# A decoder layer: retention rows scaled per token, and adaLN sums moved from the retention loop to the convolution

## The chip, the cores and the metric

One Trainium2 chip, one core. The metric is the device time of one execution in microseconds; lower is better.

## The reference

One decoder layer in float32 for 2048 tokens of 1024 channels. From a vector c come six rows of 1024 values (shift, scale, gate for each of two sub-layers), as silu(c) times a 1024 x 6144 matrix. The mixer projects the modulated input and splits it into a gated short convolution and a retention of four heads in chunks of 128 tokens; the retention's output is normalised per head, gated, set beside the convolution's, and both go through one output projection. Behind each sub-layer stands a layer norm.

```python
mod = sc @ ada_w[layer] + ada_b[layer]
shift_m, scale_m, gate_m, shift_f, scale_f, gate_f = [...]
h = x * (1.0 + scale_m) + shift_m
...
r = _head_groupnorm(_retention(q, k, v)).reshape(bsz, s, wr)
y_ret = jax.nn.silu(g) * r
return jnp.concatenate([y_conv, y_ret], axis=-1) @ w_out
...
x = _layernorm(DN_ALPHA * x + gate_m * mix, ln1_g[layer], ln1_b[layer])
h = x * (1.0 + scale_f) + shift_f
ff = _swiglu(h, w_gate[layer], w_up[layer], w_down[layer])
x = _layernorm(DN_ALPHA * x + gate_f * ff, ln2_g[layer], ln2_b[layer])
```

## The kernel before

Matrix products are taken in float16 with each operand as a high and a low part, three matmuls for one (`mm3`, lines 127 to 129). Each operand is first scaled by a power of two. `scale_of` (line 106) finds it: per-partition maxima `m` on VectorE (`absmax`, line 87), a matmul that spreads them over all partitions (`all_max`, line 99), a reduction of its result (line 104), three short steps (lines 114 to 117), and 1/s on GpSimd (line 118). `split` (lines 122 and 123) then makes the high part on ScalarE and the low part on VectorE.

The stages in order of time: a start that handles four tiles of 128 tokens while the modulation comes in; the retention loop over tiles t = 4 to 15; the convolution as twelve calls of `conv_pair` (n = 6b + u, two blocks of rows b and six units of weights u), each of 84 matmuls in seven products; the output projection with the first norm; the channel sub-layer.

In the retention loop a round t holds the four projections of tile t (`gemm_ret`), the transposes of q and k of tile t - 1 (`ret_transpose`: `split`, then two transposing DMAs on SP's queue, line 745), its scores (`ret_scores`, lines 127 to 129 at 128 columns, mask at line 759), its state (`ret_kv`, line 768), its output and norm (`ret_y`: products at lines 785 and 788, statistics on VectorE, a power and a product on GpSimd at lines 797 and 799, the gate at line 802, then the maxima), and `ret_part`, which scales and splits the result for the output projection. The scale's inverse goes to `ivr[:, t:t + 1]`, one value for each partition, which `op_half` reads as such. Also in the loop: rotary (lines 726 to 730, VectorE and GpSimd), the planes of the convolution's input (`h_more`, with eight GpSimd instructions at lines 336 to 339), and `bg_step`, twice a round.

`bg_step` does a part of the adaLN product. The matrix comes transposed in pages of 256 rows, 1 MB each; `ada_sum` (line 191) multiplies each half page with silu(c), the row `scrow`, and sums it along the row. Pages 0 to 7 (shift and scale of the mixer) are needed at the start; pages 8 to 23 are the 16 that `bg_step` takes in turn, each load one or two steps ahead of its sum. When they are done, `more_modulation` in round t = 13 adds the bias, makes rows of both gates (`row_of`, line 171) and derives the scale of the channel sub-layer. `ada_sum_pool` (line 452) is the same sum with the product on GpSimd (line 457) and the sum on ScalarE (line 462); the start uses it for two pages.

In the convolution, `cw_split` prepares the weights of unit u + 1 just before `conv_pair` of unit u in the first block: scale, scaling on ScalarE (line 873), four differences on GpSimd (874 to 877), high parts on ScalarE (881), low parts on VectorE (882); they are stored, and the second block loads them (`cw_again`).

SBUF is held as 24 pages of 8 KB a partition, taken from and given back to a list by the program (`page`, `free`); a page taken again makes its new writer wait for the last readers. The order of each engine's instructions is set ahead of time by a planner that goes through the program with costs of its own and takes the earliest traced instruction that it thinks ready (those under `tc.high_priority`, as in `scale_of`, before the others); only the start's order is written out. On the chip every engine and every DMA queue then takes its instructions in that order.

Of the kernel before, what the change touches and what calls it, by code (L numbers as in the profile page):

```python
# [40 lines left out]
def kernel(ctx: ExitStack, tc: tile.TileContext, xT, x, c, adaN, adaT, ada_b, w_ret, w_conv,  # L41
# [15 lines left out]
    def page(dt=F32, at=0):  # L57
        """8 KB a partition; at: which of the free pages, from the one that has been free for longest (0) to the one
        that has become free last (-1)"""
        t = unused.pop(max(-len(unused), min(at, len(unused) - 1)))  # L60
        v = t if dt == F32 else t.bitcast(dt)
        owner[id(v)] = (v, t)
        return v
# [25 lines left out]
    def mcol(n=1):  # L89
        """per-partition maxima, rounded to bfloat16: s leaves a factor of two up to the largest float16"""  # L90
        count[0] += 1
        return small.tile([P, n], BF16, tag=f"m{n}", name=f"m{count[0]}", bufs=4)

    def all_max(g, m, each=False, other=None):
        """g [P, 1]: the largest of m [P, n] bfloat16, on every partition; each: of every column, g [P, n]"""
# [10 lines left out]
    def scale_of(m, s, iv, each=False, room=0, other=None):  # L106
        """m: per-partition maxima; s = 2^(14 - room) / 2^floor(log2(max)), iv = 1 / s, both on every partition;
        each: one for every column of m"""
# [11 lines left out]

    def split(src, hi, lo, s):
# [3 lines left out]
    def mm3(ps, l_hi, l_lo, r_hi, r_lo, start, stop, again=False):  # L125
        """again: adds to a sum that has been read"""
# [38 lines left out]
    def row_of(cols, dst, scale):  # L165
        """dst [P, D]: the columns' values as a row on every partition, times scale"""
# [34 lines left out]
    def adan_sum(i):  # L201
        """two columns of mod as a row on the tensor engine, then turned"""
# [71 lines left out]
    def bound(mx, sh, k0=0, k1=KT):  # L274
        """a bound of |x (1 + scale) + shift| on each partition; mx: maxima of |x|, sh: of |shift|"""
# [42 lines left out]
    def h_scale():  # L318
        """one scale for the input's tiles from 8 on and for the convolution's part"""
        scale_of(bound(xall, shm), hs[:, 0:1], hs[:, 1:2], room=2)  # L320

    def h_split(src, s):
        """src: channels' tiles by a pair's 256 rows; parts by tile, by half of the channels, high and low"""
# [7 lines left out]
    def h_sums(src):  # L331
        """of the quarters A11, A12 (even tile), A21, A22: S2 for A11, S4 for A12, S3 for A21, S1 for A22, with
        S1 = A21 + A22, S2 = S1 - A11, S3 = A11 - A21, S4 = A12 - S2"""
# [7 lines left out]
    # planes for the convolution's products, in their order: A11, A12, S4, A22, S1, S2, S3  # L341
# [43 lines left out]
    def h_again(p):  # L385
        """the planes of one of the first pairs"""
# [8 lines left out]
    # The first four tiles in two groups of rows, each with its own scales, as the modulation comes in; the order in  # L395
    # which the engines take this part is that of the program.
# [8 lines left out]
    def ret_half_max(u, i):  # L405
        """unit 1 on ScalarE: sums of |w|, which are at least the maxima"""
# [15 lines left out]
    def ret_half_scale(u, i):  # L422
        """the second half gets the scale of both, the first half its own for the time being"""
# [20 lines left out]
    def ret_rescale(u):  # L444
        """the first half on the scale of both"""
# [6 lines left out]
    def ada_sum_pool(i):  # L452
        """as ada_sum, on GpSimd and ScalarE; the sums when later[i] is stepped"""
# [31 lines left out]
    def start_scale(g, p, other):  # L485
        """other: what is done while the maxima are on their way"""
# [13 lines left out]
    def start_gemm(u, g, t):  # L500
        """a third of the products at a time, those with the weights' low part last"""
# [37 lines left out]
    def in_order():  # L539
        """the engines' instructions of this block in the order in which they stand here"""  # L540
# [26 lines left out]
    with in_order():  # L567
        # some matmuls only keep the array busy until the modulation has come in, for its full clock
# [138 lines left out]
    def qk_scales(p, ivh):  # L707
        """scales that bring q and k of a pair of tiles into float16's range, whatever the products are; the scale of
        q stays on the scores, the sums and the squares that the normalisation's epsilon goes to"""
# [23 lines left out]
    def ret_transpose(t):  # L733
        """q and k, split, with the channels on the partitions, and q once more in one piece"""
# [45 lines left out]
    def ret_y(t):  # L780
# [24 lines left out]
        m = mcol()  # L805
        r = tt[:, 1536:2048]
        absmax(m, r)
        RM[t] = m

    def ret_part(t):  # L810
        r = T1[t][:, 1536:2048]
        s = col(1, "s")
        scale_of(RM.pop(t), s, ivr[:, t:t + 1])
# [29 lines left out]
    # Two tiles of columns at a time, B.1 and B.2; planes in the order of the products: B11, B21, B22, B21 - T2, T1, T2,  # L843
    # T3 with T1 = B12 - B11, T2 = B22 - T1, T3 = B22 - B12.
# [46 lines left out]
    nl, nw = [8], [8]  # L891

    def bg_step():
        if nl[0] < 24 and nl[0] <= nw[0] + 1:
            ada_load(nl[0], -1)
            nl[0] += 1
        if nw[0] < nl[0] - 1 or nl[0] == 24 and nw[0] < 24:
            ada_sum(nw[0])
            nw[0] += 1

# [1 line left out]
    gmp = []  # L902

# [954 lines left out]
```

## Time and profile before

| | us |
|---|---|
| median of 3 runs | 2157.56 |
| lowest and highest | 2155.71, 2157.85 |
| span of the profiled execution | 2156.5 |
| TensorE busy in it | 2032.1 |
| VectorE, GpSimd, ScalarE busy | 1473.8, 1015.5, 672.3 |

The span is from the first to the last instruction of one profiled execution; the profile gives no other time for that execution, so the runs' median stands for what lies around it. In the rows below PE is TensorE, PEld its weight loads, DVE VectorE, ACT ScalarE, POOL GpSimd and SP the queue that issues most DMAs; L99 is line 99 of the kernel; `<-` names what ended an idle time. A row of windows has the stretch and its length, then busy us (and instructions) of PE, PEld, DVE, ACT and POOL, then the granted clock as a share of the full one, the DMA share and GB/s.

### The profile page before, as it was taken

The page shows a single profiled execution, that of the slowest core. Times are in us where ns is not written, and L with a number is a line of the kernel's source. Part 1 is how long each engine was busy: PE and PEld are TensorE (multiplying, and loading weights), DVE is VectorE, ACT ScalarE, POOL GpSimd, SP SyncE. Part 2 cuts the span into 40 slices and gives each one's busy share as a digit, 9 for nine tenths or more (in the row PEclk, how much of TensorE's full clock was granted, in tenths as well). Part 3 has the DMA queues.
Part 4 walks back from the last instruction along what each step waited for, and adds up shares of the span by engine and source line. Part 5 has one row for each costly group of instructions (what it writes and reads, how often), then busy time and mean ns, then how long its engine had stood idle before and what let it go on. Part 6 is the DMA issues. An engine that isn't in the chain of part 4 may idle for free.

```text
span 2156.5 us, 24675 instructions
## 1 busy us (share of the span) xinstructions
PE 2032.1 (94%) x9647; PEld 952.7 (44%) x9647; DVE 1473.8 (68%) x1787; ACT 672.3 (31%) x724; POOL 1015.5 (47%) x771
## 2 busy tenths in 40 slices
PE   8899887899999998999999999999999989996998
PEld 3355444554444443344444444444444434442443
DVE  7888788777684668778655667767663483686554
ACT  5522334444321223332232333334342211212220
POOL 4554566556422477642332444545441183378234
PEclk9999999999999999999999999999999999998999
DMA  9054666496744297655211343343442745464311
GB/s 374 27 141 144 200 187 207 135 285 222 241 178 142 81 263 191 172 174 200 100 62 56 101 153 117 135 144 122 156 140 71 268 160 197 159 238 149 145 70 78
DMA packets 185429, 344.29 MB, mean 160 GB/s; under 512 B 117856, under 2 KB 117856, under 8 KB 162656
## 3 DMA queue, kind: packets, MB, share of 16 engines
q1 hardware_dynamic: 176832, 326.72, 46.2%
q10 hardware_dynamic: 8480, 15.99, 2.1%
q8 instruction: 75, 1.23, 0.2%
q14 instruction: 42, 0.34, 0.0%
HBM read 222.87 MB, written 92.54 MB: 146 GB/s over the span
## 4 chain that ended last, share of the span: by engine, by line
PE 33%; DVE 10%; POOL 8%; DMA 5%; issue 4%; ACT 2%; SPq 0%; POOLq 0%; DVEq 0%; ACTq 0%
PE ax L127 6%; PE ax L129 6%; PE ax L128 6%; PE mm L129 5%; PE mm L127 5%; PE mm L128 5%; DMA wscr<-pg 2%; ACT pg L1504 1%; DVE pg L1453 1%; DVE pg L1505 1%; DVE pg L1457 1%; DMA pg<-yscr 1%; DVE pg L1497 1%; POOL pg L1258 1%; POOL x L118 1%
## 5 line engine op out<-in xcount | busy, mean ns | idle before, releaser
L127 PE MATMUL mm<-pg,pg 128*128 128x512 f16 x1732 | 660.8, 382 | 30.7 <-ACT pg L122 19.9
L128 PE MATMUL mm<-pg,pg 128*128 128x512 f16 x1732 | 661.0, 382 | 0.0
L129 PE MATMUL mm<-pg,pg 128*128 128x512 f16 x1732 | 658.2, 381 | 1.9 <-DVE pg L882 1.0
L128 PEld LDWEIGHTS <-pg 128*128 128x128 f16 x2888 | 284.8, 99 | 362.5 <-issue 38.0
L127 PEld LDWEIGHTS <-pg 128*128 128x128 f16 x2888 | 284.7, 99 | 350.7 <-ACT pg L122 20.5
L129 PEld LDWEIGHTS <-pg 128*128 128x128 f16 x2888 | 284.6, 99 | 337.1 <-issue 5.6
L127 PE MATMUL ax<-pg,pg 128*128 128x512 f16 x1092 | 414.2, 379 | 15.0 <-DVE t2k L1440 15.0
L128 PE MATMUL ax<-pg,pg 128*128 128x512 f16 x1092 | 414.6, 380 | 0.0
L129 PE MATMUL ax<-pg,pg 128*128 128x512 f16 x1092 | 412.4, 380 | 0.0
L1449 POOL TENSOR_TENSOR pg<-pg,t2k 128x512 f32<-128x512 f32 x44 | 59.8, 1359 | 331.1 <-DVE t2k L1448 331.1
L123 DVE SCALAR_TENSOR_TENSOR pg<-pg,p2s,pg 128x2048 f16<-128x2048 f32 (+1 forms) x42 | 117.7, 2809 | 112.3 <-ACT pg L122 108.6
L122 ACT ACTIVATE pg<-pg,p2s 128x2048 f16<-128x2048 f32 (+1 forms) x42 | 77.4, 1856 | 241.4 <-PE mm L128 88.2
L87 DVE TENSOR_REDUCE m<-pg 128x2 bf16<-128x2048 f32 (+2 forms) x54 | 97.0, 1805 | 11.9 <-DMA pg<-in_w_gu_dram 8.8
L517 PE MATMUL mm<-pg,pg 128*128 128x512 f16 x384 | 89.3, 387 | 5.6 <-DVE pg L525 2.5
L1505 DVE TENSOR_TENSOR pg<-pg,pg 128x2048 f16<-128x2048 f32 (+1 forms) x22 | 49.6, 2255 | 52.8 <-ACT pg L1504 52.8
L1456 ACT ACTIVATE pg<-t2k,ivg 128x512 f32<-128x512 f32 x44 | 31.5, 716 | 151.4 <-DVE t2k L1455 151.4
L1448 DVE TENSOR_TENSOR t2k<-ax,t2k 128x512 f32<-128x512 f32 x22 | 15.2, 690 | 82.0 <-PE ax L129 82.0
L1387 ACT ACTIVATE pg<-pg 128x2048 f16<-128x2048 f32 x22 | 42.0, 1909 | 86.5 <-PE ax L128 86.5
L191 DVE SCALAR_TENSOR_TENSOR pg<-pg,pg 128x1024 f32<-128x1024 f32 x40 | 57.1, 1462 | 14.6 <-DMA pg<-in_adaT_dram 14.2
L1504 ACT ACTIVATE pg<-pg 128x2048 f16<-128x2048 f32 (+1 forms) x22 | 37.3, 1697 | 95.0 <-DMA wscr<-pg 60.5
L1558 POOL TENSOR_TENSOR pg<-pg,pg 128x2048 f32<-128x2048 f32 (+1 forms) x6 | 26.9, 4490 | 82.0 <-DMA pg<-uscr 36.4
L118 POOL TENSOR_SCALAR x<-x 128x2 f32<-128x2 f32 x22 | 37.2, 1690 | 59.7 <-DVE x L116 59.5
(273 smaller groups left out, 2893.3 us busy)
## 6 DMA issues: line engine op xcount, KB each, us to landing
pg<-wscr SPq DMA_DIRECT2D x28, 1024.0 KB, 4.9
pg<-in_w_gu_dram SPq DMA_DIRECT2D x22, 1024.0 KB, 4.8
uscr<-pg SPq DMA_DIRECT2D x44, 512.0 KB, 2.7
pg<-in_w_dn_dram SPq DMA_DIRECT2D x22, 1024.0 KB, 5.6
pg<-in_adaT_dram SPq DMA_DIRECT2D x21, 1024.0 KB, 6.5
wscr<-pg SPq DMA_DIRECT2D x77, 256.0 KB, 2.9
pg<-uscr SPq DMA_DIRECT2D x16, 1024.0 KB, 5.8
pg<-in_xT_dram SPq DMA_DIRECT2D x14, 1024.0 KB, 5.3
```

The source lines that it names most:

```text
L87: return nc.vector.tensor_reduce(dst, src, axis=AX.X, op=OP.max, apply_absolute_value=True).ins
L118: nc.gpsimd.tensor_scalar(iv, e, float(2.0 ** (room - 14)), None, op0=OP.mult)
L122: nc.scalar.activation(hi, src, AF.Copy, scale=s)
L123: nc.vector.scalar_tensor_tensor(lo, src, s, hi, op0=OP.mult, op1=OP.subtract)
L127: nc.tensor.matmul(ps, l_hi, r_hi, start=start, stop=False, skip_group_check=again)
L128: nc.tensor.matmul(ps, l_hi, r_lo, start=False, stop=False, skip_group_check=again)
L129: nc.tensor.matmul(ps, l_lo, r_hi, start=False, stop=stop, skip_group_check=again)
L191: nc.vector.scalar_tensor_tensor(v, v, 1.0, scrow, op0=OP.mult, op1=OP.mult, accum_out=mod[:, j:j + 1])
L517: nc.tensor.matmul(ps, hv[:, a, k, o], w[:, k], start=n == 0 and k == k0, stop=n == 2 and k == k1 - 1)
L1449: nc.gpsimd.tensor_add(e5, e5, p1)
L1504: nc.scalar.activation(o[:, :n, 0], src, AF.Copy)
L1505: nc.vector.tensor_sub(o[:, :n, 1], src, o[:, :n, 0])
```

## The change

Two things. First, `ret_part` no longer calls `scale_of`. The maxima of `ret_y` are kept in float32 and a new function makes a scale for each partition, that is for each token, out of its own maximum, on VectorE with 1/s on GpSimd. Second, `bg_step` is gone. The 16 pages are loaded and summed in the convolution: two loads at n = 0; in each of n = 1 to 8 one page is summed on VectorE and one on GpSimd and ScalarE, and each is followed by the load of the next but one. `more_modulation` is cut in two: the mixer's gate row at n = 3, the rest at n = 9. `crow`, the page with silu(c), is given back at n = 8 instead of in round 13. Comments were taken out too, so line numbers differ by a few.

```diff
+    def row_scale(m, s, iv):
+        nc.vector.tensor_scalar(m, m, float(2.0 ** -100), None, op0=OP.max)
+        mi = m.bitcast(I32)
+        nc.vector.tensor_scalar(mi, mi, EXPMASK, None, op0=OP.bitwise_and)
+        nc.vector.tensor_scalar(s.bitcast(I32), mi, -1.0, SBASE, op0=OP.mult, op1=OP.add)
+        nc.gpsimd.tensor_scalar(iv, m, float(2.0 ** -14), None, op0=OP.mult)
...
-        m = mcol()
-        r = tt[:, 1536:2048]
-        absmax(m, r)
+        m = col(1, "g")
+        absmax(m, tt[:, 1536:2048])
         RM[t] = m
...
-        scale_of(RM.pop(t), s, ivr[:, t:t + 1])
+        row_scale(RM.pop(t), s, ivr[:, t:t + 1])
...
-    nl, nw = [8], [8]
-
-    def bg_step():
-        if nl[0] < 24 and nl[0] <= nw[0] + 1:
-            ada_load(nl[0], -1)
-            nl[0] += 1
-        if nw[0] < nl[0] - 1 or nl[0] == 24 and nw[0] < 24:
-            ada_sum(nw[0])
-            nw[0] += 1
...
+    def ada_sum_both(i):
+        ada_sum_pool(i)
+        for _ in later.pop(i):
+            pass
+
+    def mix_modulation():
+        gmp.append(page())
+        ada_bias(16, 24)
+        row_of(mod[:, 2 * KT:3 * KT], gmp[0][:, :D], 1.0 / ALPHA)
+
     def more_modulation():
-        gmp.append(page())
-        ada_bias(16, 48)
+        ada_bias(24, 48)
         nc.vector.tensor_scalar(msc[:, 1], mod[:, 4 * KT:5 * KT], 1.0, None, op0=OP.add)
-        gm = gmp[0][:, :D]
-        row_of(mod[:, 2 * KT:3 * KT], gm, 1.0 / ALPHA)
         row_of(mod[:, 5 * KT:6 * KT], gfrow, 1.0 / ALPHA)
...
         ret_transpose(t - 1)
-        bg_step()
         gemm_ret(t, 1)
...
         ret_y(t - 1)
-        bg_step()
-        if t == NT - 3:
-            free(crow)
-            more_modulation()
...
+            if n == 0:
+                ada_load(8, -1)
+                ada_load(9, -1)
+            if 1 <= n <= 8:
+                ada_sum(6 + 2 * n)
+                if n < 8:
+                    ada_load(8 + 2 * n, -1)
+                ada_sum_both(7 + 2 * n)
+                if n < 8:
+                    ada_load(9 + 2 * n, -1)
+                else:
+                    free(crow)
+            if n == 3:
+                mix_modulation()
+            if n == 9:
+                more_modulation()
             if n == 1:
                 ret_scores(NT - 1)
```

## Rows read from the trace of the kernel before

**Rows 1.** The page: span, busy time of TensorE, its granted clock in 40 slices.

```profile
span 2156.5 us, 24675 instructions
...
PE 2032.1 (94%) x9647; PEld 952.7 (44%) x9647; DVE 1473.8 (68%) x1787; ACT 672.3 (31%) x724; POOL 1015.5 (47%) x771
...
PEclk9999999999999999999999999999999999998999
```

**Rows 2.** Windows: stretch in us, its length, busy us of each engine.

```profile
125.00:478.00 353.00, 316.26 (x1703) 175.15 (x1702) 277.71 (x510) 124.84 (x184) 189.32 (x177) 0.95 0.62 187
...
504.00:597.00 93.00, 93.00 (x445) 43.16 (x444) 62.47 (x79) 30.52 (x26) 46.81 (x45) 1.00 0.67 235
597.00:652.00 55.00, 54.91 (x258) 24.88 (x257) 46.22 (x44) 14.03 (x14) 13.13 (x14) 1.00 0.43 152
```

**Rows 3.** TensorE's waits from 125 to 478 us: releaser, total us, times, longest.

```profile
PE ax L99 <- DVE m L87: 29.2, 8, 7.1
PE ax L785 <- DVE pg L759: 6.7, 3, 4.2
```

**Rows 4.** TensorE's timeline, four places: start, us, instruction, idle time before it.

```profile
295.53 0.23 PE L99 MATMUL ax<-ident,m 128*128 128x128 f16 x1 [2.55 <-DVE m L87]
...
334.48 0.80 PE L785 MATMUL ax<-pg,pg 128*128 128x128 f32 x2 [4.16 <-DVE pg L759]
...
358.39 0.29 PE L99 MATMUL ax<-ident,m 128*128 128x128 f16 x1 [7.10 <-DVE m L87]
...
416.57 0.29 PE L99 MATMUL ax<-ident,m 128*128 128x128 f16 x1 [3.94 <-DVE m L87]
```

**Rows 5.** SP's timeline: issues of the transposes of q and k.

```profile
289.79 2.61 SPq L745 DMA_TRANSPOSE pg<-pg  x2
...
351.85 1.23 SPq L745 DMA_TRANSPOSE pg<-pg  x1
...
402.68 3.82 SPq L745 DMA_TRANSPOSE pg<-pg  x2
```

**Rows 6.** DMA issues: the median in us from issue to landing.

```profile
pg<-pg SPq DMA_TRANSPOSE x88, 3.3
```

**Rows 7.** TensorE's timeline: the same eight matmuls behind two waits.

```profile
249.57 2.02 PE L768 MATMUL ax<-pg 128*128 128x128 f32 x8
...
390.53 1.11 PE L768 MATMUL ax<-pg 128*128 128x128 f32 x8
```

**Rows 8.** VectorE's groups by line, 125 to 478 us: the adaLN sums.

```profile
L191 DVE SCALAR_TENSOR_TENSOR pg<-pg,pg 128x1024 f32<-128x1024 f32 x32 | 44.3, 1420 | 14.6 <-DMA pg<-in_adaT_dram 14.2 <-issue 0.4
```

**Rows 9.** Windows of line 104 alone, 125 to 478 us: its sum.

```profile
sum 353.00, DVE 4.96; mean DVE 4.96
```

**Rows 10.** VectorE's timeline: a sum, the mask step, one rotary line twice.

```profile
326.44 1.22 DVE L191 SCALAR_TENSOR_TENSOR pg<-pg,pg 128x1024 f32<-128x1024 f32 x1 [3.62 <-DMA pg<-in_adaT_dram]
...
333.69 0.74 DVE L759 SCALAR_TENSOR_TENSOR pg<-ax,pg,mask 128x512 f32<-128x512 f32 x1
335.90 1.76 DVE L727 TENSOR_TENSOR pg<-pg,pg 128x512 f32<-128x512 f32 x1
...
390.85 0.68 DVE L727 TENSOR_TENSOR pg<-pg,pg 128x512 f32<-128x512 f32 x1
```

**Rows 11.** GpSimd's timeline beside them.

```profile
337.07 1.72 POOL L338 TENSOR_TENSOR pg<-pg 128x512 f32<-128x512 f32 x1
```

**Rows 12.** Lines 457 and 462 alone: ns least/median/most, first and last start.

```profile
L457 POOL TENSOR_TENSOR pg<-pg,pg x4: 2354/2855/4397, 33.6 to 42.9; 128x1024 f32<-128x1024 f32 x4
...
L462 ACT ACTIVATE pg<-pg x4: 1043/1044/1047, 41.1 to 51.2; 128x1024 f32<-128x1024 f32 x4
```

**Rows 13.** Timeline: weights of the fifth unit on TensorE and VectorE, its first product.

```profile
542.75 0.28 PE L99 MATMUL ax<-ident,m 128*128 128x128 f16 x2
...
557.59 4.41 DVE L882 TENSOR_TENSOR pg<-pg,pg 128x2048 f16<-128x2048 f32 x2 [5.68 <-ACT pg L881]
...
560.99 0.38 PE L127 MATMUL mm<-pg,pg 128*128 128x512 f16 x1
```

## The prediction

> **What bounds the kernel now.** First the page's shares [rows 1]: TensorE is busy for 94% of the span, and no other engine comes near it, so time can only come out of TensorE's 124 us without work and out of stretches in which its granted clock was low. Next the stretches: the change touches the retention loop, here 125 to 478 us, and the convolution behind it, from 478 to 707 us [rows 2]. The loop is where TensorE loses: 316.3 of 353 us busy, and a mean granted clock of 0.95. In the convolution it has 93.0 of 93 us from 504 on and 54.9 of 55 us from 597 on, all at 1.00. So the loop has about 37 us of idle time to give, and the convolution has nothing to give and only something to lose.
>
> Then TensorE's waits in the loop [rows 3]. Of 36.7 us, 29.2 us in eight waits stand before line 99, the small matmul that spreads a tile's maxima over the partitions; it waits for VectorE's maximum (line 87). 6.7 us stand before line 785, the product of the scores with v, which waits for the mask step (line 759). TensorE takes its instructions in order: while line 99 stands at its head, the scores of the next tile, its state product and the next projections queue behind it, though none of them needs the maxima. The timeline has these waits one by one; three of the eight, of 2.55, 7.10 and 3.94 us, and one before line 785 stand in [rows 4].
>
> **The change, part 1: a scale per token.** It removes, for each of 16 tiles, the matmul of line 99 and the reduction of line 104. The maxima, the three short steps and GpSimd's 1/s stay, without the trip over TensorE. On TensorE the matmul itself is nothing (matmuls of its size start 0.055 us apart); on VectorE the reductions of all 18 scales in the loop are 4.96 us [rows 9], 14 of them retention tiles, so some 4 us. The gain is the wait. How much of it comes back is decided by what is late next: the scores behind line 99 need the transposed q and k.
>
> I compare, for each of the eight waits, when TensorE got to line 99 (start less idle) with when the transposes had landed: the start of the second issue plus 3.3 us [rows 5, 6]. Three cases stand in the rows. Tile 12: at 416.57 - 3.94 = 412.6; transposes by 410; all 3.94 us come back. Tile 10: at 351.3; transposes at 351.85 + 3.3 = 355.2; 7.10 - 3.9 = 3.2 us. Tile 8: at 293.0; the second of two issues that take 2.61 us from 289.79 starts at 291.1, lands at 294.4; 2.55 - 1.4 = 1.1 us. The other five, by the same two numbers, give 3.28, 4.64, 3.13, 2.33 and 1.1 us. Sum: 22.7 of 29.2 us even if nothing lands earlier. Of the other 6.5 us I count 3, since part 2 makes VectorE faster, and rotary and the splits in front of the transposes are largely VectorE's.
>
> The clock comes on top. After such a wait TensorE runs at the lower of its two levels (1.2 instead of 2.4 GHz) for a few us: the eight state products took 2.02 us after the 4.64 us wait and 1.11 us after a wait of 2.21 us [rows 7]. With the score matmuls before and the first large ones behind, I estimate 1.5 us a wait. If nine of these eleven waits go and four short ones come, 5 x 1.5 = 7.5 us return (bounds 0 and 12).
>
> **Part 2: 16 pages of adaLN sums leave the loop.** These are 32 VectorE instructions of 1.42 us mean, 44.3 us, and 14.6 us in which VectorE stood before them, 14.2 of it because the page was still being loaded [rows 8]. VectorE has 277.7 us of work in the loop [rows 2]; 44.3 and 4 come off, leaving some 229 us for a loop of about 320: it doesn't become the bound by load. One wait shows the direct effect: the mask step ran at 333.7, after VectorE had stood 3.62 us for a page and summed it for 2.4 us [rows 10], and the product of line 785 waited 4.16 us [rows 4]. I count 4.2 of the 7.0 us at that place as returned.
>
> **What is late next in the loop.** TensorE now comes earlier to each tile's scores and to line 785. In between lie rotary on VectorE and GpSimd, two splits, two transposes and the mask step. New waits are not in this trace; below they are 0, above all that was there, 29 us. I take 6.6 us, three tiles with the 2.2 us that line 785 waits on average now (6.7 / 3), since in five of eight cases the transposes had at least 1.5 us to spare and VectorE loses a sixth of its work.
>
> Retention: 22.7 + 3 + 4.2 - 6.6 + 7.5 = 31 us less.
>
> **Part 3: the sums in the convolution.** Eight pages on VectorE: 16 x 1.42 = 23 us [rows 8]. Eight on GpSimd and ScalarE: 16 multiplications at 2.85 us, 46 us, and 16 sums at 1.04 us, 17 us, on ScalarE [rows 12]. They fall in pairs 1 to 8 of the convolution, about 504 to 652 us, where VectorE has 62.5 + 46.2 = 108.7 us in 148, GpSimd 46.8 + 13.1 = 60, ScalarE 30.5 + 14.0 = 45 [rows 2]. By load it fits: about 132, 106 and 62 of 148 us. Results are read from accumulators that rotate over two sets of four banks, so a late eviction has most of a pair's 18 us. What has no such reserve is the weights of the next pair: maxima over TensorE, scale on ScalarE, four differences on GpSimd, high parts on ScalarE, low parts on VectorE. For the fifth unit this chain went from 542.75 to 562.0 us while TensorE began with it at 560.99 and needed the later planes 2.6 us on: 1.6 us to spare [rows 13]. For the sixth it was about 2, for the third and the fourth over 6. GpSimd can't drop a multiplication that it has begun: one of 2.85 us just in front of the differences costs 2.85 - 1.6 = 1.2 us, a VectorE sum in front of the low parts 1.4 us more. I take 2.5 us for each of the two short units, 1.5 us for the clock and 0.5 us for the eight small matmuls that make the gate row, which TensorE now meets between two pairs, where they can wait for the last sum: 7 us (0 below; above see the third rival).
>
> The 16 loads of 1 MB move too. On SP's queue each one takes the page of a sum just finished, so SP stands until that sum is done, with weight loads, stores and plane loads behind it. The loop is rid of this; in the convolution the next unit's weights are fetched a pair ahead, 18 us, and I count nothing. If that cover is gone it is the wait for the page, one pair of multiplications, 5.7 us, once or twice. The last modulation values, now behind pair 8, are read only after pair 11: no cost.
>
> The Trainium skill (SBUF — State Buffer, the section on the three doors of SBUF) says that a VectorE instruction with two SBUF inputs and a GpSimd instruction that reads SBUF take a port pair as a lock, and the later one stands until the other is done. In this trace the rotary product of 128x512 took 0.68 us at 390.85 and 1.76 us at 335.90, beside GpSimd differences of about that length [rows 10, 11], which agrees.
>
> **Sum.** 31 - 7 = 24 us less. The profiled execution shows a span of 2156.5 us and no time beside it; the median of the runs is 2157.56, about 1 us more. 2156.5 - 24 + 1 = 2133.
>
> **Rivals.** *All comes back.* The transposes come early as soon as VectorE is relieved, and the convolution hides everything: 29.2 + 7.0 + 10 of clock = 46 us, 2111. For it: only 225 us of VectorE work; against it: three transposes landed only after TensorE had come, a fourth 1.5 us before.
> *Another wait takes its place.* The chain from q and k over rotary, GpSimd and SP to the scores keeps the period that it has now, (416.57 - 295.53) / 4 = 30 us between these tiles [rows 4]; new waits are 25 us instead of 6.6 and the clock returns nothing: 31 - 18.4 - 7.5 = 5 us less in the loop, 7 more behind it: 2160, no measurable change or a little slower. For it: GpSimd's differences for the input planes stand in front of rotary's two steps.
> *The convolution becomes bound by VectorE and GpSimd* (slower). Place: units two to six and the evictions around them. If every VectorE instruction stands for the whole of each multiplication, pairs 1 to 5 need 62.5 + 14 + 28 = 105 us in 93 and pairs 6 to 8 need 46 + 9 + 17 = 72 in 55: 29 us more, and eight waits with 1.5 us of clock each, 12: 41 us against 31, 2167. It decides from 31 us on, four a pair. For it: the lengthened instructions above; against it: reductions and reads of the accumulators kept their time beside GpSimd, and GpSimd was idle for most of pairs 5 to 8. The lock that the skill describes would give just this case if no instruction found a gap.
>
> **How the numbers follow.** Forecast 0.58, with a range of its own of 2120 to 2150; all back 0.15; another wait 0.13; convolution bound 0.14. The predicted time is 2133. The range goes from 2113, close to the case in which all comes back, to 2159, at the second rival; what it leaves out is most of the third one and the ends of the others. Within 0.2% (4.3 us, about what a measurement of this kernel can tell from no change) is 2153.2 to 2161.9. Faster takes the forecast and the first rival with a little of the second, 0.75; same most of the second, 0.11; slower the third, 0.14.
>
> **What would show it.** Right: no retention tile in line 99's waits, TensorE's idle time in the loop at 10 to 15 us, the loop 25 to 38 us shorter, its granted clock at 0.97 or more; in the convolution a few us of waits for the low parts of weights at units five and six, and everything behind it unchanged but earlier. Wrong: waits before the scores for the transposes of 2 us in most tiles, or more than 15 us of new idle time between the convolution's pairs. A different order of the pages in the later stages could move their stalls by a few us either way; nothing in these rows tells its sign.

## The result and the profile after

The changed kernel takes 2171.38 us (median of 4 runs, 2169.69 to 2172.29) against 2157.70 us for the kernel before beside it: a ratio of 1.0063, 95% interval 1.005 to 1.0077. It is slower, by 0.6%; 2133 with a range of 2113 to 2159 was forecast. The profiled execution took 2169.69 us with a span of 2167.9.

All runs are read by the same two places on TensorE's timeline: the first product of the convolution's pair 1 (the first 512-wide matmul into the second set of accumulators), and the first small matmul of `row_of` with `msc`, right behind the convolution.

| us | pair 1 starts | from there to the rows | behind | span |
|---|---|---|---|---|
| before | 504.27 | 202.5 | 1449.8 | 2156.5 |
| after | 474.89 | 245.5 | 1447.5 | 2167.9 |
| difference | -29.4 | +43.0 | -2.3 | +11.4 |

So the loop gave what was forecast (31), and the convolution took 43 where 7 were forecast. The pairs begin at other times in the two kernels, so they are set side by side here from product to product, 84 large matmuls a pair (stretch, length, busy us of PE, PEld, DVE, ACT, POOL, granted clock, DMA share, GB/s). Before, pairs 1 to 5 and from pair 6 to the rows:

```profile
504.27:597.40 93.13, 93.13 (x445) 43.11 (x443) 62.60 (x80) 30.52 (x26) 46.81 (x45) 1.00 0.67 237
597.40:706.72 109.32, 109.23 (x511) 49.65 (x510) 71.70 (x72) 24.13 (x24) 27.77 (x29) 1.00 0.45 159
```

After, the loop, then pairs 1 to 5, from pair 6 to the rows, and both together:

```profile
125.00:478.00 353.00, 329.69 (x1783) 177.73 (x1782) 237.77 (x450) 133.73 (x189) 193.29 (x192) 0.97 0.56 165
...
474.89:609.50 134.61, 106.30 (x460) 45.98 (x458) 116.93 (x119) 50.90 (x63) 113.50 (x65) 0.91 0.72 269
609.50:720.42 110.92, 110.92 (x529) 51.51 (x528) 70.63 (x78) 25.64 (x26) 23.79 (x28) 1.00 0.46 171
474.89:720.42 245.53, 217.22 (x987) 97.49 (x985) 187.55 (x197) 76.54 (x89) 137.29 (x92) 0.95 0.60 225
```

Pairs 1 to 5 take 134.6 us instead of 93.1, with 116.9 us of work on VectorE instead of 62.6 and 113.5 on GpSimd instead of 46.8. From pair 6 on it is nearly as it was, 110.9 instead of 109.3. From pair 1 to the rows TensorE stood 28.3 us (0.1 before), and its work took 217.2 us instead of 202.4. Of these 14.8 us more, 4.0 are the 32 small matmuls that make the two gate rows: the change took them from the loop, where they were busy for 3.9 us, to the convolution, and the prediction has them in neither. The other 10.8 go with a mean granted clock of 0.95 instead of 1.00.

TensorE's waits after, first in the loop, then from 474 to 620 us (releaser, total us, times, longest):

```profile
PE ax L793 <- DVE pg L767: 15.4, 4, 9.7
PE ax L136 <- DMA pg<-pg: 7.1, 2, 6.8
...
PE ax L137 <- DVE pg L889: 8.3, 5, 2.7
PE mm L135 <- ACT pg L888: 4.5, 1, 4.5
PE ax L135 <- ACT pg L888: 4.1, 3, 2.6
PE mm L137 <- DVE pg L889: 3.7, 2, 2.1
```

Lines 888 and 889 are the high and low parts of the next unit's weights (881 and 882 before); these four rows are 20.6 of the 28.3 us. The costliest groups of VectorE and GpSimd from 440 to 740 us (last numbers: busy us, mean ns):

```profile
L465 POOL TENSOR_TENSOR pg<-pg,pg 128x1024 f32<-128x1024 f32 x16 | 51.4, 3231 | 0.1
L199 DVE SCALAR_TENSOR_TENSOR pg<-pg,pg 128x1024 f32<-128x1024 f32 x16 | 34.2, 2166 | 0.0
L889 DVE TENSOR_TENSOR pg<-pg,pg 128x1536 f16<-128x1536 f32 x6 | 19.2, 3194 | 0.0
L889 DVE TENSOR_TENSOR pg<-pg,pg 128x2048 f16<-128x2048 f32 x6 | 19.0, 3164 | 12.7 <-ACT pg L888 12.7
```

The same two lines alone: shortest, median and longest ns, first and last start:

```profile
L199 DVE SCALAR_TENSOR_TENSOR pg<-pg,pg x16: 1211/2277/3367, 487.9 to 582.1; 128x1024 f32<-128x1024 f32 x16
L465 POOL TENSOR_TENSOR pg<-pg,pg x16: 2342/3326/4417, 471.7 to 586.6; 128x1024 f32<-128x1024 f32 x16
```

Two things are to be seen. The planner put all 16 pages between 471.7 and about 591 us, in the end of pair 0 and in pairs 1 to 5; pairs 1 to 8 were forecast. And there the instructions of VectorE and GpSimd lengthen each other: the sums take 2166 ns instead of 1420 [rows 8], the products 3326 in the median instead of 2855 [rows 12], and the low parts 3164 and 3194 where the groups of the kernel before have 2702 and 1750. The sixth unit's weights show it (VectorE's, GpSimd's and TensorE's timeline; x2 is two instructions in one row):

```profile
579.91 2.29 DVE L199 SCALAR_TENSOR_TENSOR pg<-pg,pg 128x1024 f32<-128x1024 f32 x1
582.13 2.27 DVE L199 SCALAR_TENSOR_TENSOR pg<-pg,pg 128x1024 f32<-128x1024 f32 x1
584.34 8.25 DVE L889 TENSOR_TENSOR pg<-pg,pg 128x2048 f16<-128x2048 f32 x2
...
583.29 7.68 POOL L465 TENSOR_TENSOR pg<-pg,pg 128x1024 f32<-128x1024 f32 x2
...
588.82 0.39 PE L137 MATMUL ax<-pg,pg 128*128 128x512 f16 x1 [2.07 <-DVE pg L889]
```

For the fifth unit of the kernel before both low parts took 4.41 us together [rows 13]; here they took 8.25, beside a page's two products of 7.68, which alone are 2 x 2.34, and TensorE waited.

### The profile page after: what moved, and what is told of

The parts are those of the page before. It is cut to its first block, busy times and chain, and to the rows that moved or that the text cites. A ratio compares the mean times of both kernels' runs of the same rounds, so it can differ in the third digit from the quotient of the medians.

```text
span 2167.9 us, 24641 instructions
## 1 busy us (share of the span) xinstructions
PE 2029.9 (94%) x9631; PEld 945.6 (44%) x9631; DVE 1464.4 (68%) x1740; ACT 691.0 (32%) x756; POOL 1063.1 (49%) x787
## 4 chain that ended last, share of the span: by engine, by line
PE 30%; DVE 11%; POOL 10%; DMA 5%; issue 4%; ACT 3%; SPq 0%; POOLq 0%; DVEq 0%; ACTq 0%
PE ax L135 5%; PE ax L136 5%; PE ax L137 5%; PE mm L137 4%; PE mm L135 4%; PE mm L136 4%; DMA wscr<-pg 2%; ACT pg L1520 2%; DVE pg L1469 1%; DVE pg L1521 1%; DVE pg L1473 1%; DMA pg<-yscr 1%; DVE pg L1513 1%; POOL pg L1274 1%; POOL pg L1398 1%
## 5 line engine op out<-in xcount | busy, mean ns | idle before, releaser
L135 PE MATMUL mm<-pg,pg 128*128 128x512 f16 x1732 | 659.6, 381 | 36.6 <-ACT pg L130 18.9
L131 DVE SCALAR_TENSOR_TENSOR pg<-pg,p2s,pg 128x2048 f16<-128x2048 f32 (+1 forms) x42 | 117.0, 2793 | 113.1 <-ACT pg L130 112.9
L87 DVE TENSOR_REDUCE m<-pg 128x2 bf16<-128x2048 f32 (+1 forms) x38 | 86.3, 2276 | 8.9 <-DMA pg<-in_w_gu_dram 6.4
L131 DVE SCALAR_TENSOR_TENSOR pg<-pg,hs,pg 128x1024 f16<-128x1024 f32 x32 | 53.1, 1678 | 26.3 <-ACT pg L130 26.1
L737 POOL TENSOR_TENSOR pg<-pg 128x512 f32<-128x512 f32 x16 | 24.8, 1548 | 85.8 <-DVE pg L736 71.0
```

The costliest lines, as they stand in the source:

```text
L87: return nc.vector.tensor_reduce(dst, src, axis=AX.X, op=OP.max, apply_absolute_value=True).ins
L131: nc.vector.scalar_tensor_tensor(lo, src, s, hi, op0=OP.mult, op1=OP.subtract)
L135: nc.tensor.matmul(ps, l_hi, r_hi, start=start, stop=False, skip_group_check=again)
```

## The experiments

Times are medians; each ratio is to the kernel before on the same chip, with its 95% interval. "Convolution" is the stretch from pair 1 to the rows.

**The two halves of the change.** First the scale per token alone, `bg_step` kept as before:

```diff
...
-        scale_of(RM.pop(t), s, ivr[:, t:t + 1])
+        row_scale(RM.pop(t), s, ivr[:, t:t + 1])
```

> Only the scale per token; the adaLN sums stay in the retention loop as before. If the wait before line 99 was the loop's loss: 22.7 us of waits and some 5 of clock come back, less a few new ones, 2132 to 2140 us, with the convolution at its old length (504 to 707, 203 us between the first product of unit 1 and the rows behind pair 11). If the loop needed the sums gone as well (VectorE late for rotary and the mask): 2148 to 2157 us, with the waits moved from line 99 to lines 785 and the transposes.

2162.07 us, 1.0016 (1.0006 to 1.0027): the loop ends at 506.24, 2.0 us later than before, convolution 203.4. Neither of the two expected times was met. Then the reverse, the sums moved as in the change and the scale per tile kept:

```diff
...
-        row_scale(RM.pop(t), s, ivr[:, t:t + 1])
+        scale_of(RM.pop(t), s, ivr[:, t:t + 1])
```

> Only the sums moved; the scale goes over TensorE as before. If the convolution's loss comes from the sums alone: the same 43 us more there, and in the loop only what VectorE's relief gives (5 to 12 us): 2187 to 2195 us. If the loop's 29 us came mainly from the sums' leaving: 2165 to 2175 us.

2167.49 us, 1.0045 (1.0032 to 1.0058): the loop ends at 477.67, 26.6 us earlier; convolution 239.8. So nearly the whole gain of the loop comes with the sums' leaving (3.9 us of it are the rows' small matmuls). Some of it is what part 1 had counted on, since line 99 waits 16.9 us here from 125 to 478 instead of 29.2:

```profile
PE ax L99 <- DVE m L87: 16.9, 8, 4.0
```

TensorE's waits in the loop with the scale alone show why it gave nothing, and under them VectorE's and TensorE's timelines show one of them:

```profile
PE ax L792 <- DVE pg L766: 27.2, 7, 9.2
PE mm L178 <- ACT pg L708: 7.5, 1, 7.5
```

The timelines:

```profile
359.46 1.22 DVE L198 SCALAR_TENSOR_TENSOR pg<-pg,pg 128x1024 f32<-128x1024 f32 x1 [5.38 <-DMA pg<-in_adaT_dram]
...
362.42 0.74 DVE L766 SCALAR_TENSOR_TENSOR pg<-ax,pg,mask 128x512 f32<-128x512 f32 x1
...
363.21 0.80 PE L792 MATMUL ax<-pg,pg 128*128 128x128 f32 x2 [4.89 <-DVE pg L766]
```

The waits for line 99 are gone (29.2 us in [rows 3]), and the product behind the mask waits 27.2 us instead of 6.7. VectorE stands 5.38 us for a page that is still being loaded, sums it, and only then makes the mask, for which TensorE waits. VectorE took the mask in its queue's order, behind the page.

**What in the convolution costs the 43 us.** Four kernels keep the change's loop and all 16 loads and leave out sums (so the modulation's later values are not computed in them): the pages only loaded and given back; only VectorE's eight summed; only GpSimd's and ScalarE's eight summed; and all as in the change but each product replaced by three memsets of the same page.

```diff
-                ada_sum(6 + 2 * n)
+                ada_drop(6 + 2 * n)
...
-                ada_sum_both(7 + 2 * n)
+                ada_drop(7 + 2 * n)
...
-            nc.gpsimd.tensor_mul(v, v, scrow)
+            if i < 8:
+                nc.gpsimd.tensor_mul(v, v, scrow)
+            else:
+                for _ in range(3):
+                    nc.gpsimd.memset(v, 0.0)
```

> As the changed kernel, but the 16 pages are only loaded and given back, none is summed, and those modulation values stand at zero: what is left out are the sums. If the sums' time on VectorE and GpSimd makes the loss: the convolution is back at 203 us, 2125 to 2132 us. If the loads on SP's queue or the three pages fewer make it: 20 us or more of the 43 stay, 2145 us or more.

> As the changed kernel, but the eight pages of GpSimd and ScalarE are only loaded (their values stand at zero); the eight of VectorE are summed. Loads alone left the convolution at 207.5 us, with GpSimd's half it took 223.3, with both 245.5. If the halves hurt by being there together (VectorE's two-input instructions and GpSimd's products lengthening each other): VectorE's half alone costs under 8 us, its sums take 1.2 to 1.5 us, the convolution 208 to 215 us, 2131 to 2140 us in all. If VectorE's own queue is the cost: about 22 us more than loads alone, the convolution at 225 to 230 us, 2148 to 2156 us.

> As the changed kernel, but the eight pages of VectorE are only loaded, not summed (their values stand at zero); the eight of GpSimd and ScalarE are summed. If GpSimd's products are the main cost, by their own time in front of the weights' differences and by lengthening VectorE's instructions: 25 to 35 of the 43 us stay, 2152 to 2163 us. If VectorE's own sums are (34 us of its queue): 10 to 15 us stay, 2138 to 2145 us.

> As the changed kernel, but each of the sixteen products on GpSimd is replaced by three memsets of the same half page, which read nothing (what is left out is the product, the sums of those pages are zero); GpSimd's place in its queue stays taken for a similar time. If reading by both engines at once lengthens the instructions: VectorE's sums go back from 2.2 to 1.2 to 1.5 us, the low parts of the weights from 3.0 and 3.3 to about 2.3 and 1.8, and the convolution to 215 to 228 us. If GpSimd's products hurt by standing in front of the weights' differences: the convolution stays at 238 us or more.

| | us, ratio (interval) | pair 1 starts | convolution | stood |
|---|---|---|---|---|
| loads alone | 2136.58, 0.9897 (0.9871 to 0.9922) | 475.70 | 207.5 | 1.5 |
| VectorE's half | 2146.79, 0.9943 (0.9923 to 0.9962) | 476.30 | 221.0 | 10.9 |
| GpSimd's half | 2150.70, 0.9964 (0.9949 to 0.9979) | 474.72 | 223.3 | 12.3 |
| memsets for products | 2147.65, 0.9946 (0.9927 to 0.9966) | 476.57 | 220.2 | 10.0 |
| the change | 2171.38, 1.0063 (1.005 to 1.0077) | 474.89 | 245.5 | 28.3 |

With the loads alone the convolution is 5.0 us longer than before, and hardly by the loads: the rows' small matmuls are in it for 3.9 us, and TensorE stood 1.5. Over this run VectorE's half costs 13.5, GpSimd's 15.8 (each between the times of its two theories), and both together 38.0, which is 8.7 more than their sum. That alone would show little, since two kernels with nearly the same work differ by 9.0 us there (below). The run with memsets shows more. GpSimd is nearly as busy in it (43.7 us of memsets for 51.4 of products), in the same place of its queue; this run's groups on GpSimd and VectorE from 440 to 740 us:

```profile
L469 POOL MEMSET pg<- 128x1024 f32 x48 | 43.7, 948 | 3.2 <-DMA pg<-in_adaT_dram 3.1
...
L199 DVE SCALAR_TENSOR_TENSOR pg<-pg,pg 128x1024 f32<-128x1024 f32 x16 | 24.4, 1554 | 3.4 <-DMA pg<-in_adaT_dram 3.4
...
L893 DVE TENSOR_TENSOR pg<-pg,pg 128x2048 f16<-128x2048 f32 x6 | 14.6, 2429 | 10.2 <-ACT pg L892 10.2
L893 DVE TENSOR_TENSOR pg<-pg,pg 128x1536 f16<-128x1536 f32 x6 | 12.2, 2041 | 0.5 <-ACT pg L892 0.5
```

With VectorE's half and ScalarE's sums kept too it costs no more than VectorE's half alone, 220.2 against 221.0. So 25.3 us of the change's loss, well above what an order alone made here, come with the products' reading beside VectorE, not with GpSimd being taken when the weights' differences want it: with memsets a sum takes 1554 ns in the mean and the low parts 2429 and 2041, with products 2166, 3164 and 3194.

Would the pages be cheap on VectorE alone, then?

```diff
-                ada_sum_both(7 + 2 * n)
+                ada_sum(7 + 2 * n)
```

> As the changed kernel, but all sixteen pages are summed on VectorE, none on GpSimd and ScalarE. Lengthening theory: 32 sums at 1.25 to 1.5 us, 40 to 48 us more on VectorE in pairs 1 to 8 and GpSimd as before; the convolution 212 to 225 us, 2135 to 2150 us, faster than the changed kernel. VectorE's queue theory: twice its half, the convolution at 245 us or more, no better than the changed kernel.

2170.65 us, 1.0053 (1.0033 to 1.0073), convolution 244.2. Without one product on GpSimd it loses as much. Its pairs 1 to 5:

```profile
476.08:609.30 133.22, 102.07 (x459) 46.30 (x457) 117.03 (x148) 33.13 (x31) 71.80 (x49) 0.90 0.78 283
```

TensorE's three largest waits in its convolution:

```profile
PE ax L135 <- ACT pg L888: 13.3, 3, 7.0
PE ax L137 <- DVE pg L889: 8.6, 4, 5.5
PE mm L179 <- DVE t2k L975: 5.5, 1, 5.5
```

A sum is shorter here (1575 ns), but there are 32, and VectorE is busy for 117.0 of 133.2 us, as in the change (116.9 of 134.6). So lengthened instructions are how the change fills VectorE in these pairs, and more instructions fill it as well. GpSimd is stretched too: with none of the sums' work it is busy for 71.8 us, against 53.4 in these pairs with the loads alone, and its differences come ahead of the high parts for which TensorE waits longest here. What is scarce by these runs is the two engines' time in pairs 1 to 5.

**The sums later.** In pairs 6 to 8 VectorE and GpSimd have room [rows 2]. First load behind the sixth unit's store, four pages a pair in pairs 5 to 8, the gate row at n = 6:

```diff
-            if 1 <= n <= 8:
-                ada_sum(6 + 2 * n)
...
+            if 5 <= n <= 8:
+                for i in (4 * n - 12, 4 * n - 10):
+                    if i == 8:
+                        with tc.issue_after(cw_last[0]):
+                            ada_load(8, -1)
+                            ada_load(9, -1)
+                    ada_sum(i)
...
```

> As the changed kernel, but the first two of the sixteen loads wait in SP's queue for the store of the sixth unit's weights, and the sums are written in pairs 5 to 8, two pages on VectorE and two on GpSimd and ScalarE in each; the gate row at pair 6. Nothing is left out. If the loss lies in the preparation of the weights (pairs 1 to 5): the convolution 203 to 210 us, 2128 to 2140 us. If VectorE and GpSimd are short of time in the second block too: waits of the products for evictions there, 220 us or more, 2145 us or more.

2172.57 us, 1.0065 (1.0049 to 1.0082), convolution 246.3: no better. The waits for weights are gone, and one new wait is 20.3 us long:

```profile
PE mm L179 <- DVE mod L224: 21.6, 2, 20.3
```

It stands before small matmuls of `row_of`, which the planner put between two pairs and which need the last sums. I took them for the mixer's gate row and held those behind pair 8's last product, with `more_modulation` at n = 10 and the weights of the output projection a pair later:

```diff
-            if n == 6:
-                mix_modulation()
+            if n == 9:
+                with tc.issue_after(pe_last[0]):
+                    mix_modulation()
```

> The sums in pairs 5 to 8, as in the run before, but the gate row and what needs it two to six pairs later, its small matmuls queued on TensorE behind the ninth pair. Theory 1 (in the run before, the 21.6 us wait for the gate row's small matmuls and some waits behind it ate what the quiet pairs gave): convolution about 246 - 22 = 224 us instead of 246, idle time in it 12 us or less, 2148 to 2152. Theory 2 (sums by both engines cost the convolution about 40 us in any place, since VectorE's two-input instructions and GpSimd's products stretch each other everywhere): convolution still 240 us or more, 2165 to 2172.

2156.04 us, 0.9996 (0.9987 to 1.0005), convolution 227.6; a wait of 11.5 us stays there. It was the other row, that of the channel sub-layer, so its call was held too, behind pair 10:

```diff
-            if n == 10:
-                more_modulation()
+            if n == 11:
+                with tc.issue_after(pe_last[0]):
+                    more_modulation()
```

> As the run with the held gate row, but the second group of small matmuls (the channel sub-layer's row, one wait of 11.5 us in that run) is queued behind the eleventh pair as well. Theory 1 (the late sums cost little by themselves; that wait was the rest): the wait is gone, convolution 214 to 218 us, 2141 to 2146, faster than the kernel before. Theory 2 (the wait moves to the next place that needs the last sums, behind the convolution): 2153 to 2157.

2149.20 us, 0.996 (0.9945 to 0.9975), convolution 222.9, the wait gone: faster than both kernels, by 0.4% and about 1%. The forecast of 2141 to 2146 was missed, since 14.2 us of standing remain in other places. Pairs 1 to 5 take 93.1 us again, as before the change; the 20.4 us that the convolution still costs (4 of them the rows' small matmuls) lie in pairs 6 to 11, so the quiet pairs don't take the sums for nothing. The same with the scale per tile:

> As the run beside it, but with one scale for a tile as in the kernel before, so it has the sums' move alone, late. Theory 1 (the scale per token returns nothing, as the first run with it alone showed): within 4 us of the run beside it, 2138 to 2146. Theory 2 (the forecast's part 1: with the sums gone the wait for line 99 is what is left): 15 us or more above the run beside it, waits for line 99 of 15 us or more.

2159.46 us, 1.0005 (0.9996 to 1.0015). The loop ends 1.4 us later than in the run beside it, so the scale per token again returns next to nothing there; but the convolution is 9.0 us longer, though the two differ there in hardly more than the last tile's scale. TensorE stands 18.1 us in it instead of 14.2, 5.2 of them before a gate row's small matmuls, and from pair 6 to the rows its granted clock is 0.91 instead of 0.97. In the change itself the sign was the other way (239.8 with the scale per tile, 245.5 without). Why the planner's orders differ so stays open. A half-way version, eight pages on VectorE in the loop and eight on VectorE in pairs 5 to 8:

> Scale per token kept; eight pages (8 to 15) summed on VectorE in the retention loop, one a round, the other eight on VectorE in pairs 5 to 8, none on GpSimd, the gate row in round 13 as in the kernel before. Theory 1 (VectorE's time in the loop costs about 1.7 us of TensorE's wait a page, 26.6 us for 16; pairs 5 to 8 have the room, and GpSimd's products were the worse half): loop 13 us shorter than before, convolution 0 to 8 us longer, 2145 to 2153. Theory 2 (a page costs the same 1.7 us wherever VectorE sums it): loop 13 shorter, convolution 13 longer, 2156 to 2160. Theory 3 (the loop's waits need all sums gone before they fall): loop unchanged, 2160 or more.

2158.15 us, 1.0005 (0.9994 to 1.0016): the loop 9.6 us shorter than before, the convolution 9.9 longer, nearest to the second theory.

**What in the loop gave the 29 us.** The scale per token, the sums left in the loop, and each page loaded one step further ahead, so that VectorE should not stand for it:

```diff
-        if nl[0] < 24 and nl[0] <= nw[0] + 1:
+        while nl[0] < 24 and nl[0] <= nw[0] + 2:
...
-        if nw[0] < nl[0] - 1 or nl[0] == 24 and nw[0] < 24:
+        if nw[0] < nl[0] - 2 or nl[0] == 24 and nw[0] < 24:
```

> Scale per token, sums stay in the retention loop, but each page is loaded one step further ahead of its sum. Theory 1 (the wait that took line 99's place in the run with the scale alone is VectorE standing for a page, 21 us before its sums there, with the mask queued behind): VectorE's idle time before the sums falls under 8 us, the wait for the mask from 27 to under 12 us, the loop 12 to 25 us shorter, 2135 to 2150, with the convolution as before. Theory 2 (it is the time of the sums themselves, 44 to 51 us of VectorE): less than 5 us shorter, 2155 to 2162.

The same edit in the kernel before, and the scale per token with each load going to the page that has been free longest (`ada_load(nl[0])`):

> The kernel before with one edit: each page is loaded one step further ahead. If VectorE's standing for pages (14 us) delays the maxima for line 99 too, 5 to 14 us shorter, 2143 to 2152; if line 99's waits are the length of the chain alone, 2155 to 2160.

> Scale per token, sums in the loop, loads as far ahead as before, but each takes the page that has been free longest instead of the one freed last, so that its load need not wait for that page's last readers. If the loads are late because the queue waits for the page: VectorE's idle time before the sums falls under 10 us and the time to 2140 to 2152; if they are late because they are issued late: no change, 2158 to 2162.

Then two steps further ahead, and one step with the oldest page:

> As the run with the scale per token and loads one step further ahead, now two steps further. If the rest of VectorE's standing for pages (15.5 us there) is what still holds the mask: standing under 8 us, loop 5 to 10 us shorter again, 2138 to 2143. If the loads are issued late whatever the step (SP's queue, the page's last readers): standing and time as in that run, 2145 to 2149.

> Loads one step further ahead and into the page that has been free longest, scale per token, sums in the loop. If the two causes of late loads add up: standing under 8 us, loop 17 to 21 us shorter than before, 2136 to 2141. If they are one and the same: 2145 to 2151.

| sums in the loop | us, ratio (interval) | VectorE stood for pages | product waited for the mask | pair 1 starts |
|---|---|---|---|---|
| scale per token, loads as before | 2162.07, 1.0016 (1.0006 to 1.0027) | 21.1 | 27.2 | 506.24 |
| one step ahead | 2147.62, 0.9946 (0.9927 to 0.9965) | 15.5 | 18.9 | 494.23 |
| oldest page | 2151.13, 0.9966 (0.9952 to 0.9979) | 19.3 | 12.0 | 497.24 |
| two steps ahead | 2148.48, 0.9951 (0.9936 to 0.9966) | 9.8 | 14.1 | 495.10 |
| one step, oldest page | 2150.99, 0.9965 (0.9953 to 0.9978) | 12.0 | 11.6 | 498.27 |
| scale per tile, one step ahead | 2157.37, 0.9988 (0.9977 to 1.0) | 14.2 | | 505.61 |

The same loads do nothing for the time with the scale per tile, where VectorE stood as long as before (14.2 us); with the scale per token the other loads shorten the loop by 8 to 12 us. But the standing does not set the size. In none of the runs did it fall under the 8 or 10 us of the theories; a fall from 15.5 to 9.8 leaves the loop as it is; and with the oldest page it is still 19.3, with the loop 9.0 us shorter. What counts is what stands in front of a mask that TensorE waits for. In the run with the scale alone, four of the seven waits for the mask (14.7 of 27.2 us) have a sum in front that stood for its page, as in the timelines above. Before the longest, 9.16 us, VectorE stood for none:

```profile
323.26 1.56 DVE L198 SCALAR_TENSOR_TENSOR pg<-pg,pg 128x1024 f32<-128x1024 f32 x1
324.75 2.27 DVE L198 SCALAR_TENSOR_TENSOR pg<-pg,pg 128x1024 f32<-128x1024 f32 x1
326.95 2.27 DVE L198 SCALAR_TENSOR_TENSOR pg<-pg,pg 128x1024 f32<-128x1024 f32 x1
...
329.22 2.20 DVE L198 SCALAR_TENSOR_TENSOR pg<-pg,pg 128x1024 f32<-128x1024 f32 x1
...
331.35 0.74 DVE L766 SCALAR_TENSOR_TENSOR pg<-ax,pg,mask 128x512 f32<-128x512 f32 x1
```

So the other loads return up to 12 us. Of the other 19 that the loop gains without the sums (494.23 to 474.89), 4.8 are the rows' small matmuls and 3.4 a wait in front of them, both in the run with loads one step ahead; for the rest the sums' own time on VectorE fits, but no run here removes that alone, nor the loads alone.

## Why the prediction was wrong, step by step

*TensorE bounds the kernel, and the convolution has only something to lose*: right, and the case decided by it.

*Part 1, 25.7 us of line 99's waits back*: wrong. Alone it gave -2.0. The estimate compared each wait with the landing of q and k, and there time was to be had; it left out that the mask, for which the next product waits, stands in VectorE's queue behind the sums, some of which wait for their pages. In the second rival's words another wait took its place, though not over rotary and the transposes. *Part 2, 4.2 us*: mis-sized, 26.6 by itself, 3.9 of it the rows' small matmuls, which no term has. Otherwise its row was there: 44.3 us of sums and 14.2 of standing for pages [rows 8]; I counted only those waits of TensorE that named the mask, but the same queue also delays the maxima, for which line 99 waits (29.2 us before, 16.9 without the sums). *New waits of 6.6 us*: the loop after has 15.4 for the mask and 7.1 for transposes. *Clock, +7.5*: the granted clock of the loop rose from 0.95 to 0.97, in the direction forecast; its share was not separated. The sum, 31, was met by 29.4 through other terms than those it was made of, which is luck.

*Part 3, 7 us*: this is the step that failed; the convolution took 43 us more, 36 beyond the forecast. Its mis-sized terms are two. The durations were taken from rows in which the other engine was mostly not reading: 23 us of sums became 34.2 and 46 us of products 51.4, and the weights' low parts, not counted as lengthened at all, went from 26.7 (six of 2702 and of 1750 ns) to 38.2. And the place was taken from the loop over n, pairs 1 to 8, where the planner took them as soon as pages were there, all by 591 us. Over pairs 1 to 8, 148 us, the load fits; but pairs 1 to 5 have 93 us of TensorE's work, and VectorE was busy for 116.9 us in them and GpSimd for 113.5. *Two short units*: TensorE's seven waits for low parts and four for high parts fall on more units than these, from 476 to 593 us. *The loads cost nothing*: nearly right, 1.5 us of standing in the run with the loads alone. *The gate row's small matmuls, 0.5 us*: a wait of 0.8 in the change, and 20.3 and 11.5 us before the other row when the sums came late. *Behind the convolution unchanged*: -2.3 us, right.

The third rival is what happened: 29 us of waits and 12 of clock were worked out, 28.3 of standing and 10.8 of clock were measured, 2167 us against 2171. That the sizes agree so well is luck in part: it had ten pages in pairs 1 to 5 for 12 us of the 29 and the rest in pairs 6 to 8, while all 16 were summed by pair 5 and TensorE stood in pairs 1 to 5 alone. What spoke against it, that GpSimd was idle in most of pairs 5 to 8, was true, but the planner put the sums ahead of these. Its mechanism is shown in the main: products cost 25.3 us more than memsets in their place. It counted a whole product for each VectorE instruction, and the low parts came close to that: 8.25 us for two beside 7.68 us of products, against 4.41 without them.

## What to carry to other kernels

Work moved into a stage is priced by that stage's queues: look at where the planner will put it, not where the loop has it, and at the engine with the least room there, with the durations that its instructions have beside the newcomers. When a wait is to be removed, first ask what stands in front of the next thing that the bound engine needs, in that other engine's queue; here an instruction that stood for a load held back the mask, so that one half of the change returned nothing until the loads were earlier. And small matmuls that read a late result stop everything behind them, so queue them where the result is surely there.

## What the runs showed of the hardware

A sum of 128x1024 on VectorE took 1.21 us by itself in the changed kernel, a product of 128x1024 on GpSimd 2.34. Of the 16 sums 14 took longer, 1.50 to 3.37 us, and each of the 14 ended 1.08 to 1.09 us after the end of the GpSimd instruction beside which it had begun. For four of them, the longest among them, that was a product; for the other ten it was an instruction of 128x512, most often one of the weights' differences, so nine of the ten that took 2.27 to 2.29 us stood for such a one and not for a product. In the same way ten of the 16 products took 2.81 to 4.42 us, and each ended 2.20 to 2.22 us after the end of the VectorE instruction beside which it had begun, six times a low part. GpSimd's and VectorE's timelines show one case of each kind of wait of a sum:

```profile
486.91 3.33 POOL L465 TENSOR_TENSOR pg<-pg,pg 128x1024 f32<-128x1024 f32 x1
487.95 3.37 DVE L199 SCALAR_TENSOR_TENSOR pg<-pg,pg 128x1024 f32<-128x1024 f32 x1
...
521.74 2.25 POOL L881 TENSOR_TENSOR pg<-pg 128x512 f32<-128x512 f32 x1
522.79 2.28 DVE L199 SCALAR_TENSOR_TENSOR pg<-pg,pg 128x1024 f32<-128x1024 f32 x1
```

The product ended at 490.24 and the sum at 491.32; the difference ended at 523.99 and the sum at 525.07. The Trainium skill (SBUF — State Buffer, SBUF: two separate sides) says that the two engines take a port pair as a lock for the whole of an instruction, and the one that comes later stands until then. The trace agrees, with the 1.08 and 2.20 us above: neither engine went on until the other's instruction was over. The Trainium skill (SBUF — State Buffer, SBUF: two separate sides) limits this, for a VectorE instruction with two inputs from SBUF, to GpSimd instructions that read SBUF. The run with memsets agrees: three sums that had nothing but memsets beside them took 1.21 to 1.22 us.
